# Sliding-window attention inside a decoder block: both key blocks of a query tile folded into one square per head

## The chip, the core and the metric

The kernel runs on one core of a Trainium2 chip. The metric is the device time of one launch in microseconds (us); the median of three runs of the kernel before is 1155.35 us (1154.95 to 1155.95). The core has five engines with a queue each, worked in order: PE (matrix products; PEld is its weight load), DVE (vector), ACT (scalar, activations), POOL (general vector work, SBUF only) and SP (issues DMAs). An instruction waits at the head of its queue until the semaphores that it names are reached, and everything behind it waits with it.

## What is computed

A decoder block on x of 1024 x 1024 in float32: RMSNorm, an input projection, a pooling mixer beside a sliding-window attention, gates, output projections and an MLP. The change lies in the attention alone:

```python
s = einsum('bnqhgd,bnkhd->bnhgqk', qb, kk) * scale      # kk: previous block and own block, 256 keys
rel = qi + BLOCK - kj                                   # BLOCK = WINDOW = 128
s = where((rel >= 0) & (rel < WINDOW) & has_prev, s, NEG_INF)
p = softmax(concatenate([s, sink], -1))[..., :-1]
o = einsum('bnhgqk,bnkhd->bnqhgd', p, vv)
```

There are 8 tiles of 128 queries, 8 query heads of width 64, and 2 key/value heads. A query in row q of its tile sees keys q+1 to 127 of the previous block and keys 0 to q of its own: 128 keys at most, and for every key column j exactly one of the two blocks is visible.

## The kernel before

Every float32 operand of a matrix product is split into a high and a low part (`split`, L99: ACT copies the high part at L100, DVE or POOL subtracts at L101), and a product is three passes of parts (`PASSES`). Engine order is not written out by hand: a scheduler places the instructions by priority and readiness, and the tiles of a pool (a tag with so many buffers) add the waits for reuse.

The attention stage runs from about 45 to 154 us of the span. The loop at L489 goes over the query tiles n = 0 to 7 and works on two groups g of four heads each. For each (n, g):

- `score` (L279): 12 matmuls at L296 put the scores of four heads, 256 keys wide, into the two banks of tag "sc", of which there is one buffer. Four fused DVE instructions (L303) add the mask, scale and negate, write SBUF, and give the row minimum.
- `attend` (L307): ACT makes four exponentials with row sums (L318), DVE adds the sink, inverts and normalises all 4 x 256 columns (L322). PE transposes each head in two halves (L328: 8 transposes for n > 0, 4 for n = 0). For each key/value head ACT and DVE split the transposed 128 x 512 into parts (`pt`, L330). Twelve matmuls (L335) form the output, and ACT copies it out (L338).

Around it stand: `qkv_tile` (L340), the projections of tile n + 4 for n < 4 (L172, L178); `pre_qkv` (L242), which moves that projection out of PSUM on DVE (L247, L248) and applies the rotation on POOL (L255 to L258, "the rotation" below); `post_qkv` (L260), five transposes (L265, L266) and the splits of queries, keys and values, the values' subtraction on POOL; `make_rb` (L352), eight small matmuls; and `pool_u` (L509), whose 128 x 512 matmuls at L517 depend on nothing in the attention and are what the scheduler puts between the attention's matmuls once the projections have run out ("fillers" below). A stage later, at L703, POOL adds two 128 x 512 tiles in SBUF.

Of the kernel before, what the change touches and what calls it, by code (L numbers as in the profile page):

```python
# [8 lines left out]
F32 = mybir.dt.float32  # L9
F32R = mybir.dt.float32r  # L10
AF = mybir.ActivationFunctionType
ALU = mybir.AluOpType
AX = mybir.AxisListType

P = 128
S = 1024
# [4 lines left out]
NEG = -1e30  # L21
WINDOWS = (2, 4, 8, 16)
NH = 8
HD = 64
# [2 lines left out]
F = 4096  # L27
NF = F // P
HEAD_ORDER = (0, 4, 1, 5, 2, 6, 3, 7)


PASSES = ((0, 0), (0, 1), (1, 0))
# [3 lines left out]
C_MASK = C_ID + P  # L36
# [14 lines left out]
def block_kernel(ctx: ExitStack, tc, xt, x, consts, vecs, sinks, b_qkv, g_post, g_mlp, g_mlp_post,  # L51
                 w_qkv, w_u, w_g, w_pool, w_bp, w_ba, w_o, w_up, w_dn, x1_dram, spill, f_dram, out):
    nc = tc.nc
    act, dve, pool, pe = nc.scalar, nc.vector, nc.gpsimd, nc.tensor

    cp = ctx.enter_context(tc.tile_pool(name="cp", bufs=1))
# [11 lines left out]
    def nm(s):  # L68
        cnt[0] += 1
        return f"{s}_{cnt[0]}"  # L70
# [13 lines left out]
    def at(tag, bufs, shape, dt=F32):  # L84
        return ap_.tile([P] + shape, dt, tag=tag, name=nm(tag), bufs=bufs)

    def bank(tag, shape=None):
        return psum["pool"].tile([P] + (shape or [512]), F32, tag=tag, name=nm(tag), bufs=psum["bufs"][tag])
# [7 lines left out]
    def f32(ap):  # L96
        return ap.bitcast(F32)

    def split(hi, lo, src, eng=dve):  # L99
        act.copy(hi, src)  # L100
        eng.tensor_tensor(lo, src, f32(hi), ALU.subtract)  # L101
# [42 lines left out]
    cst = cp.tile([P, C_N], F32, name="cst")  # L144
    vec = cp.tile([P, V_N], F32, name="vec")
    snk = cp.tile([P, NH], F32, name="snk")
    nsnk = cp.tile([P, NH], F32, name="nsnk")
# [5 lines left out]
    warm = small(1, "warm")  # L153
    act.activation(warm, eps, AF.Identity)
    ident = cst[:, C_ID:C_ID + P]
    mask = cst[:, C_MASK:C_MASK + 2 * P]

    def bcast(src, n):
        t = bcp.tile([P, 1024], F32, tag="bc", name=nm("bc"))
# [23 lines left out]
    bq = {0: bq01[:, 0, :], 1: bq01[:, 1, :], 2: bank("mm"), 3: bank("mm")}  # L183
    bkv = {0: bank("at", [2, 256]), 2: bank("at", [2, 256])}
    bss = bank("at", [NT])
    sq = at("qkv", 2, [S])
    ones = vec[:, V_ONE:V_ONE + 1]
    for k in range(NK):
        xs = at("s4", 4, [S])
# [10 lines left out]
        q = wslot([2, 512]) if k < 6 else ga_.tile([P, 2, 512], F32R, tag="ga", name=nm("wq"))  # L200
        if k % 2 == 0:
            wkv.append(ga_.tile([P, 2, 2, 256], F32R, tag="ga", name=nm("wkv")))
        kv = wkv[-1]
        for th, t in enumerate(halves_):
            c = slice(th * 512, (th + 1) * 512)
# [24 lines left out]

    khi = at("khi", 1, [S], F32R)
    klo = at("klo", 1, [S], F32R)
    vs = {}
    y = [[None, None], [None, None]]
    for th in range(2):
        for kh in range(2):
# [3 lines left out]
    tfs = {}  # L240

    def pre_qkv(n):  # L242
        tf = y[1][n - 2].rearrange("p a b -> p (a b)") if n in (2, 3) else at("qkv", 2, [1024])
        tfs[n] = tf
        t = tf[:, :768].rearrange("p (h d) -> p h d", d=HD)
        rn = r1[:, n:n + 1]
        dve.scalar_tensor_tensor(tf[:, :512], bq[n], rn, bq_b[:, :512], ALU.mult, ALU.add)  # L247
        dve.scalar_tensor_tensor(tf[:, 512:768], bkv[n // 2 * 2][:, n % 2, :], rn, bq_b[:, 512:768], ALU.mult, ALU.add)  # L248
        c = cst[:, C_COS + 8 * n:C_COS + 8 * n + 8].unsqueeze(1).unsqueeze(1).broadcast_to([P, 10, 2, 8])
        s = cst[:, C_SIN + 8 * n:C_SIN + 8 * n + 8].unsqueeze(1).unsqueeze(1).broadcast_to([P, 10, 2, 8])  # L250
        rot = t[:, :10, :ROT].rearrange("p h (a b) -> p h a b", a=2)
        a = tf[:, 768:928].rearrange("p (h a b) -> p h a b", a=2, b=8)
        b = sp.tile([P, 10, 2, 8], F32, tag="rb", name=nm("rb"), bufs=1)
        eng = pool if n else dve
        eng.tensor_tensor(a, rot, c, ALU.mult)  # L255
        eng.tensor_tensor(b, rot, s, ALU.mult)
        eng.tensor_tensor(rot[:, :, 0, :], a[:, :, 0, :], b[:, :, 1, :], ALU.subtract)
        eng.tensor_tensor(rot[:, :, 1, :], a[:, :, 1, :], b[:, :, 0, :], ALU.add)  # L258

    def post_qkv(n):  # L260
        tf = tfs.pop(n)
        t = tf[:, :768].rearrange("p (h d) -> p h d", d=HD)
        bt, bk = (bank("at" if n < 2 else "mm") for _ in range(2))
        for m in range(4):
            pe.transpose(bt[:, m * P:(m + 1) * P], tf[:, m * P:(m + 1) * P], ident)  # L265
        pe.transpose(bk[:, :P], tf[:, 512:640], ident)  # L266
        qt = at("qt", 2, [2, 512], F32R)
        split(qt[:, 0, :], qt[:, 1, :], bt)
        ks = slice(n * P, (n + 1) * P)
        split(khi[:, ks], klo[:, ks], bk[:, :P])  # L270
        vt = at("v", 4, [2, 3, HD], F32R)
        pool.memset(f32(vt[:, :, 1, :]), 0.0)
        split(vt[:, 0, ::2, :], vt[:, 1, ::2, :], t[:, 10:12, :], pool)
        vs[n] = vt.rearrange("p l a d -> p l (a d)")
        qts[n] = qt

    scores, soft = {}, {}

    def score(n, g):  # L279
        qt = qts[n]  # L280
        k0 = max(n - 1, 0) * P
        nk = 2 * P if n else P
        msk = mask[:, 2 * P - nk:]
        s4 = at("s4", 4, [4, 256])
        if g == 0:
            soft[n] = tuple(sp.tile([P, NH], F32, tag=t, name=nm(t)) for t in ("nmx", "es", "den"))
        nmx = soft[n][0]
        sb = bank("sc", [2, 2, 256])

        with tc.high_priority():  # L290
            for i in range(2):
                m = 2 * g + i
                for j, (qx, kx) in enumerate(((0, klo), (1, khi), (0, khi))):
                    for kv in range(2):
                        r = slice(kv * HD, (kv + 1) * HD)
                        pe.matmul(sb[:, kv, i, :nk], qt[r, qx, m * P:(m + 1) * P], kx[r, k0:k0 + nk],  # L296
                                  start=j == 0, stop=j == 2)

        for i in range(2):
            for kv in range(2):  # L300
                j = 2 * i + kv
                h = 4 * g + j
                dve.tensor_tensor_reduce(s4[:, j, :nk], sb[:, kv, i, :nk], msk, -HD ** -0.5, nsnk[:, h:h + 1],  # L303
                                         ALU.add, ALU.min, nmx[:, h:h + 1])
        scores[n, g] = s4

    def attend(n, g):  # L307
        k0 = max(n - 1, 0) * P
        nkb = 2 if n else 1
        nk = nkb * P  # L310
        s4 = scores.pop((n, g))
        nmx, es, den = soft[n]
        gs = slice(4 * g, 4 * g + 4)
        dve.tensor_tensor(es[:, gs], snk[:, gs], nmx[:, gs], ALU.add)
        act.activation(es[:, gs], es[:, gs], AF.Exp)
        for j in range(4):
            h = 4 * g + j
            act.activation(s4[:, j, :nk], s4[:, j, :nk], AF.Exp, scale=-1.0, bias=nmx[:, h:h + 1],  # L318
                           accum_out=den[:, h:h + 1])
        dve.tensor_tensor(den[:, gs], den[:, gs], es[:, gs], ALU.add)  # L320
        dve.reciprocal(den[:, gs], den[:, gs])
        dve.tensor_tensor(s4[:, :, :nk], s4[:, :, :nk], den[:, gs].unsqueeze(2).broadcast_to([P, 4, nk]), ALU.mult)  # L322
        pts = []
        for kv in range(2):
            b = bank("at", [2, 2 * P])
            for kb in range(nkb):
                for i in range(2):
                    pe.transpose(b[:, kb, i * P:(i + 1) * P], s4[:, 2 * i + kv, kb * P:(kb + 1) * P], ident)  # L328
            pt = at("pt", 2, [2, 2, 2 * P], F32R)
            split(pt[:, 0, :nkb], pt[:, 1, :nkb], b[:, :nkb])  # L330
            pts.append(pt)
        yb = bank("at", [2, P])
        mms = [(kv, kb, j) for kv in range(2) for kb in range(nkb) for j in PASSES]
        for j, (kv, kb, (vh, ph)) in enumerate(mms):
            pe.matmul(yb.rearrange("p m q -> p (m q)"), vs[k0 // P + kb][:, vh, kv * HD:kv * HD + P],  # L335
                      pts[kv][:, ph, kb, :], start=j == 0, stop=j == len(mms) - 1)
        c = (n % 4) * P
        act.copy(y[n // 4][g][:, :, c:c + P], yb)  # L338

    def qkv_tile(n):  # L340
        bq[n] = bank("mm")
# [189 lines left out]
    d = {}  # L531
# [464 lines left out]
    sq = sp.tile([P, 2, NT], F32, tag="fsq", name="fsq", bufs=1)  # L996
# [90 lines left out]
    u, v, c11, c12 = acc4("u"), acc4("v"), acc4("c11"), acc4("c12")  # L1087
# [5 lines left out]
    for j, (i, s_) in enumerate(steps):  # L1093
# [12 lines left out]
        for t in range(4):  # L1106
# [18 lines left out]
            else:  # L1125
                n = 4 + t
# [18 lines left out]
def _layout(inputs):  # L1145
    a = {k: np.asarray(v) for k, v in inputs.items()}
    f = np.float32
    c = np.ascontiguousarray
    w_in, b_in = a["w_in"][0], a["b_in"][0]
    q = w_in[:, 512:1024].reshape(D, NH, HD)[:, HEAD_ORDER, :].reshape(D, 512)  # L1150
    bq = b_in[512:1024].reshape(NH, HD)[list(HEAD_ORDER)].reshape(512)

# [4 lines left out]
    x = a["x"][0]  # L1157
    consts = np.zeros((P, C_N), f)
    consts[:, C_ID:C_ID + P] = np.eye(P, dtype=f)
    rel = np.arange(P)[:, None] + P - np.arange(2 * P)[None, :]  # L1160
    consts[:, C_MASK:C_MASK + 2 * P] = np.where((rel >= 0) & (rel < P), 0.0, NEG)
    inv = f(THETA) ** (-np.arange(0, ROT, 2, dtype=f) / f(ROT))
    ang = np.arange(S, dtype=f)[:, None] * inv[None, :].astype(f)
    for col, t in ((C_COS, np.cos(ang)), (C_SIN, np.sin(ang))):
# [11 lines left out]
        ("x", x.reshape(NT, P, D)),  # L1176
        ("consts", consts),
        ("vecs", c(vecs)),
        ("sinks", c(a["attn_sinks"][0][list(HEAD_ORDER)])),
        ("b_qkv", c(np.concatenate([bq, b_in[1024:1280]]))),  # L1180
        ("g_post", a["g_mix_post"][0]),
        ("g_mlp", a["g_mlp_pre"][0]),
# [30 lines left out]
```

## Time and profile before

| | |
|---|---|
| median of 3 runs | 1155.35 us |
| the profiled execution's own time | 1155.82 us |
| its span, first to last instruction | 1154.0 us |
| mean granted PE clock over the span | 0.996 |
| PE idle in 40 to 160 us, by windows of 20 us | 2.13, 0.22, 0.73, 0.88, 0.21, 0.05 us |
| POOL busy in 60 to 160 us | 9.1 us of 100 |

A row of the page's groups gives line, engine, operation, output<-input, shape and count, then the busy time, the mean of one in ns, and the idle time of the engine just before them with what ended it. A row of the windows gives the busy time of each engine in a stretch and the granted PE clock as a share of full speed. A matmul's record lasts until its result is out, so that records overlap; what one costs PE's queue is the spacing of starts, which the timeline shows.

### The profile page before, as it was taken

What the parts mean: (1) busy time and instruction counts of PE and PEld (TensorE: products, weight loads), DVE (VectorE), ACT (ScalarE), POOL (GpSimd) and SP (SyncE); (2) the same over time, 40 slices, a digit from 0 to 9 for tenths busy, and PEclk for the clock granted to TensorE, in tenths of its full rate; (3) what the DMA queues carried; (4) which work ended last, traced back from release to release, by engine and by line L of the source; (5) the groups of instructions that cost most, each with busy time, mean ns of one, the idle gap of its engine ahead of it and who ended that gap; (6) DMA issues with size and microseconds to landing.
All of it is one profiled execution on the core that took longest, in us unless ns stands there. A gap on an engine that the chain in (4) does not pass through costs nothing.

```text
span 1154.0 us, 14409 instructions
## 1 busy us (share of the span) xinstructions
PE 1131.8 (98%) x5356; PEld 937.4 (81%) x5356; DVE 826.6 (72%) x1339; ACT 535.0 (46%) x927; POOL 49.1 (4%) x66
## 2 busy tenths in 40 slices
PE   7999999999999999999999999999999999999997
PEld 6878888788888887888788888888888888888885
DVE  7787979888654584776997766666657945446887
ACT  7465845544332233464655444444444345344342
POOL 3410100000000150000000000000000000000000
PEclk9999999999999999999999999999999999999999
DMA  7101243544345453333255434343788665432652
GB/s 263 62 1 55 75 144 119 187 170 147 121 169 184 149 198 110 128 128 128 91 219 215 160 145 163 139 169 133 263 302 285 218 198 175 135 93 73 201 189 104
DMA packets 66167, 179.10 MB, mean 155 GB/s; under 512 B 6193, under 2 KB 6193, under 8 KB 66097
## 3 DMA queue, kind: packets, MB, share of 16 engines
q1 hardware_dynamic: 60336, 157.73, 40.3%
q10 hardware_dynamic: 5760, 20.45, 4.6%
q8 instruction: 42, 0.69, 0.2%
q14 instruction: 29, 0.23, 0.1%
HBM read 127.82 MB, written 50.33 MB: 154 GB/s over the span
## 4 chain that ended last, share of the span: by engine, by line
PE 88%; DVE 5%; ACT 4%; DMA 2%; issue 1%; SPq 0%; DVEq 0%; ACTq 0%
PE mm L436 20%; PE at L436 16%; PE at L1051 14%; PE mm L1051 11%; PE mm L768 5%; PE mm L373 5%; PE mm L517 4%; PE mm L172 3%; PE mm L375 2%; PE at L335 2%; PE sc L172 1%; PE at L178 1%; PE sc L296 1%; ACT s L318 1%; PE at L328 1%
## 5 line engine op out<-in xcount | busy, mean ns | idle before, releaser
L1051 PE MATMUL at<-ar,wh 128*128 128x512 f32 x744 | 169.6, 389 | 0.0
L1051 PEld LDWEIGHTS at<-ar,wh 128*128 128x128 f32 x744 | 139.6, 188 | 29.4 <-DVE ar L101 0.4
L1051 PE MATMUL mm<-ar,wh 128*128 128x512 f32 x576 | 131.0, 389 | 0.0
L100 ACT CAST wh<-st 128x512 fp32r<-128x512 f32 (+1 forms) x106 | 67.4, 643 | 128.9 <-PE mm L436 39.3
L1051 PEld LDWEIGHTS mm<-ar,wh 128*128 128x128 f32 x576 | 108.1, 188 | 22.5
L101 DVE TENSOR_TENSOR wh<-raw,wh 128x1024 fp32r<-128x1024 f32 x53 | 64.9, 1224 | 82.0 <-ACT wh L100 81.9
L100 ACT CAST wh<-raw 128x1024 fp32r<-128x1024 f32 x53 | 55.9, 1055 | 133.5 <-PE at L1051 61.8
L101 DVE TENSOR_TENSOR wh<-st,wh 128x512 fp32r<-128x512 f32 (+1 forms) x106 | 83.1, 789 | 19.8 <-ACT wh L100 17.4
L436 PE MATMUL mm<-gr,wh 128*128 128x512 f32 x300 | 72.4, 391 | 0.1
L436 PE MATMUL mm<-T,wx 128*128 128x512 f32 x288 | 67.5, 389 | 0.0
L436 PEld LDWEIGHTS mm<-gr,wh 128*128 128x128 f32 x300 | 56.0, 188 | 12.0 <-ACT g L833 0.5
L436 PEld LDWEIGHTS mm<-T,wx 128*128 128x128 f32 x288 | 54.1, 188 | 11.2
L436 PE MATMUL at<-T,wx 128*128 128x512 f32 x252 | 59.1, 389 | 0.0
L436 PEld LDWEIGHTS at<-T,wx 128*128 128x128 f32 x252 | 47.3, 188 | 9.8
L436 PE MATMUL mm<-x,wh 128*128 128x512 f32 x216 | 51.4, 391 | 0.5 <-ACT g L443 0.5
L101 DVE TENSOR_TENSOR ar<-B,ar 128x1024 fp32r<-128x1024 f32 x37 | 45.1, 1220 | 6.2 <-ACT ar L100 6.2
L436 PEld LDWEIGHTS mm<-x,wh 128*128 128x128 f32 x216 | 40.3, 188 | 9.7 <-ACT g L443 1.1
L517 PE MATMUL mm<-x,wh 128*128 128x512 f32 x192 | 47.7, 393 | 0.0
L436 PE MATMUL at<-gr,wh 128*128 128x512 f32 x183 | 44.4, 389 | 0.0
L100 ACT CAST ar<-B 128x1024 fp32r<-128x1024 f32 x37 | 38.8, 1050 | 7.9 <-DVE s L850 3.2
L685 DVE TENSOR_TENSOR g<-g,mm 128x512 f32<-128x512 f32 x32 | 20.5, 683 | 28.7 <-PE mm L375 28.6
L517 PEld LDWEIGHTS mm<-x,wh 128*128 128x128 f32 x192 | 35.4, 188 | 6.5
(345 smaller groups left out, 2243.2 us busy)
## 6 DMA issues: line engine op xcount, KB each, us to landing
raw<-f_dram SPq DMA_DIRECT2D x53, 512.0 KB, 3.7
f_dram<-g SPq DMA_DIRECT2D x30, 512.0 KB, 3.3
B<-in_w_dn_dram SPq DMA_DIRECT2D x24, 512.0 KB, 5.8
st<-in_w_up_dram SPq DMA_DIRECT2D x22, 512.0 KB, 3.8
f_dram<-g ACTq DMA_DIRECT2D x17, 512.0 KB, 2.6
st<-in_w_g_dram SPq DMA_DIRECT2D x16, 512.0 KB, 3.7
g<-spill_dram SPq DMA_DIRECT2D x16, 512.0 KB, 4.5
raw<-in_w_dn_dram SPq DMA_DIRECT2D x16, 512.0 KB, 4.6
```

Of the source, the lines that this page charges most:

```text
L100: act.copy(hi, src)
L101: eng.tensor_tensor(lo, src, f32(hi), ALU.subtract)
L172: pe.matmul(bq, xs_[k][n // 4][:, xh, n % 4 * P:(n % 4 + 1) * P], wq[k][:, h, :], start=k == 0 and j == 0, stop=k == NK - 1 and j == 2)
L178: pe.matmul(bkv[n // 2 * 2][:, n % 2, :], xs_[k][n // 4][:, xh, n % 4 * P:(n % 4 + 1) * P], wkv[k // 2][:, h, k % 2, :], start=k == 0 and ...
L335: pe.matmul(yb.rearrange("p m q -> p (m q)"), vs[k0 // P + kb][:, vh, kv * HD:kv * HD + P], pts[kv][:, ph, kb, :], start=j == 0, stop=j == ...
L373: pe.matmul(bs[th], whi[:, k, :], rhs(k, hl, th), start=k == 0 and hl == 0, stop=False)
L375: pe.matmul(bs[th], wlo[:, k, :], rhs(k, 0, th), start=False, stop=k == nk - 1)
L436: pe.matmul(b, w[:, wh, kt, :], xo[kt][:, xh, :], start=not after and kt == 0 and j == 0, stop=kt == 3 and j == 2, skip_group_check=after)
L517: pe.matmul(b, (whi, wlo)[h][:, k, :], xr(k, xh, th), start=k == 0 and j == 0, stop=k == NK - 1 and j == 2)
L685: dve.tensor_tensor(z[:, sl], z[:, sl], bs[th], ALU.mult)
L768: pe.matmul(obs[n][dj], l, wos[k][whl][:, dj * 512:(dj + 1) * 512], start=k == 0 and hl == 0 and whl == 0, stop=k == NK - 1 and hl == 1)
L1051: pe.matmul(bs[t], fo[fh][:, k2, t * P:(t + 1) * P], wo_[wh][:, k2, :], start=not after and s2 == 0 and k2 == 0 and j == 0, stop=s2 == NS ...
```

## The change

The scores of both blocks are still computed, 256 wide. Then ACT copies the own block's 4 x 128 columns out of PSUM, and one DVE instruction (`copy_predicated`) overwrites the columns above the diagonal with those of the previous block (for n = 0 with a constant). From there on each head has one square of 128 x 128: a row maximum and its scaling on DVE, the exponentials on 128 columns, one normalisation of 4 x 128 columns, four transposes and one split. The output is formed as p times the previous block's values, plus (p masked to the own block) times (own values minus previous values). The masked copies `pc` of both parts are made by two POOL multiplications of 128 x 512, and the difference `dvs` is made and split on POOL and ACT in `post_qkv`. The number of matmuls into the output stays 12 (6 for n = 0); they stand in the order p high, p low, pc high, pc low. The order of heads inside a group, the constants and some buffer counts follow suit.

```diff
-    mask = cst[:, C_MASK:C_MASK + 2 * P]
+    from_prev = cst[:, C_MASK:C_MASK + P].bitcast(mybir.dt.uint32)
+    own_t = cst[:, C_MASK + P:C_MASK + 2 * P]
+    neg = cp.tile([P, 1], F32, name="neg")
+    dve.memset(neg, NEG)
...
     def post_qkv(n):
...
+        if n:
+            dt_ = at("dv", 3, [2, 3, HD], F32R)
+            dv = tf[:, 768:896].rearrange("p (a d) -> p a d", d=HD)
+            pool.tensor_tensor(dv, t[:, 10:12, :], tfs.pop(n - 1)[:, 640:768].rearrange("p (a d) -> p a d", d=HD),
+                               ALU.subtract)
+            pool.memset(f32(dt_[:, :, 1, :]), 0.0)
+            split(dt_[:, 0, ::2, :], dt_[:, 1, ::2, :], dv, pool)
+            dvs[n] = dt_.rearrange("p l a d -> p l (a d)")
...
     def score(n, g):
...
-        s4 = at("s4", 4, [4, 256])
+        s4 = at("sc4", 4, [4, P])
...
-        for i in range(2):
-            for kv in range(2):
-                j = 2 * i + kv
-                h = 4 * g + j
-                dve.tensor_tensor_reduce(s4[:, j, :nk], sb[:, kv, i, :nk], msk, -HD ** -0.5, nsnk[:, h:h + 1],
-                                         ALU.add, ALU.min, nmx[:, h:h + 1])
+        heads = sb.rearrange("p a b k -> p (a b) k")
+        act.copy(s4, heads[:, :, nk - P:nk])
+        prev = heads[:, :, :P] if n else neg.unsqueeze(1).broadcast_to([P, 4, P])
+        dve.copy_predicated(s4, from_prev.unsqueeze(1).broadcast_to([P, 4, P]), prev)
+        gs = slice(4 * g, 4 * g + 4)
+        dve.tensor_reduce(nmx[:, gs], s4, AX.X, ALU.max)
+        dve.scalar_tensor_tensor(nmx[:, gs], nmx[:, gs], -SCALE, nsnk[:, gs], ALU.mult, ALU.min)
...
-            act.activation(s4[:, j, :nk], s4[:, j, :nk], AF.Exp, scale=-1.0, bias=nmx[:, h:h + 1],
-                           accum_out=den[:, h:h + 1])
+            act.activation(s4[:, j], s4[:, j], AF.Exp, scale=SCALE, bias=nmx[:, h:h + 1], accum_out=den[:, h:h + 1])
...
-        dve.tensor_tensor(s4[:, :, :nk], s4[:, :, :nk], den[:, gs].unsqueeze(2).broadcast_to([P, 4, nk]), ALU.mult)
-        pts = []
-        for kv in range(2):
-            b = bank("at", [2, 2 * P])
-            for kb in range(nkb):
-                for i in range(2):
-                    pe.transpose(b[:, kb, i * P:(i + 1) * P], s4[:, 2 * i + kv, kb * P:(kb + 1) * P], ident)
-            pt = at("pt", 2, [2, 2, 2 * P], F32R)
-            split(pt[:, 0, :nkb], pt[:, 1, :nkb], b[:, :nkb])
-            pts.append(pt)
+        dve.tensor_tensor(s4, s4, den[:, gs].unsqueeze(2).broadcast_to([P, 4, P]), ALU.mult)
+        b = bank("at", [4, P])
+        for j in range(4):
+            pe.transpose(b[:, j], s4[:, j], ident)
+        pt = at("s4", 4, [2, 4, P], F32R)
+        split(pt[:, 0], pt[:, 1], b)
+        pc = None
+        if n:
+            pc = at("s4", 4, [2, 4, P], F32R)
+            for h in range(2):
+                pool.tensor_tensor(pc[:, h], f32(pt[:, h]), own_t.unsqueeze(1).broadcast_to([P, 4, P]), ALU.mult)
+        probs[n, g] = pt, pc
+
+    def attend_v(n, g):
+        pt, pc = probs.pop((n, g))
         yb = bank("at", [2, P])
-        mms = [(kv, kb, j) for kv in range(2) for kb in range(nkb) for j in PASSES]
+        parts = ((vs[n - 1], pt), (dvs[n], pc)) if n else ((vs[0], pt),)
+        mms = [(v, p, kv, j) for v, p in parts for kv in range(2) for j in PASSES]
+        mms.sort(key=lambda e: (e[1] is pc, e[3][1]))
```

More of the change, by code (lines that the diff above doesn't have):

```diff
@@ L29 @@
 HEAD_ORDER = (0, 4, 1, 5, 2, 6, 3, 7)
+SOFT_ORDER = (0, 1, 4, 5, 2, 3, 6, 7)
 PASSES = ((0, 0), (0, 1), (1, 0))
@@ L185, in block_kernel @@
     bss = bank("at", [NT])
-    sq = at("qkv", 2, [S])
+    sq = at("qkv", 4, [S])
     ones = vec[:, V_ONE:V_ONE + 1]
@@ L232, in block_kernel @@
     klo = at("klo", 1, [S], F32R)
-    vs = {}
+    vs, dvs = {}, {}
     y = [[None, None], [None, None]]
@@ L242, in pre_qkv @@
     def pre_qkv(n):
-        tf = y[1][n - 2].rearrange("p a b -> p (a b)") if n in (2, 3) else at("qkv", 2, [1024])
+        tf = y[1][n - 2].rearrange("p a b -> p (a b)") if n in (2, 3) else at("qkv", 4, [1024])
         tfs[n] = tf
@@ L260, in post_qkv @@
     def post_qkv(n):
-        tf = tfs.pop(n)
+        tf = tfs[n]
         t = tf[:, :768].rearrange("p (h d) -> p h d", d=HD)
@@ L275, in post_qkv @@
         qts[n] = qt
+        if n:
[6 more added lines that the diff above has]
+            dvs[n] = dt_.rearrange("p l a d -> p l (a d)")
     scores, soft = {}, {}
+    SCALE = HD ** -0.5
     def score(n, g):
@@ L282, in score @@
         nk = 2 * P if n else P
-        msk = mask[:, 2 * P - nk:]
-        s4 = at("s4", 4, [4, 256])
+        s4 = at("sc4", 4, [4, P])
         if g == 0:
@@ L297, in score, with attend_t @@
                                   start=j == 0, stop=j == 2)
-        for i in range(2):
-            for kv in range(2):
-                j = 2 * i + kv
-                h = 4 * g + j
-                dve.tensor_tensor_reduce(s4[:, j, :nk], sb[:, kv, i, :nk], msk, -HD ** -0.5, nsnk[:, h:h + 1],
-                                         ALU.add, ALU.min, nmx[:, h:h + 1])
+        heads = sb.rearrange("p a b k -> p (a b) k")
[5 more added lines that the diff above has]
+        dve.scalar_tensor_tensor(nmx[:, gs], nmx[:, gs], -SCALE, nsnk[:, gs], ALU.mult, ALU.min)
         scores[n, g] = s4
[L307 to L310, printed above, removed]
+    probs = {}
+    def attend_t(n, g):
         s4 = scores.pop((n, g))
@@ L334, in attend @@
-        for j, (kv, kb, (vh, ph)) in enumerate(mms):
-            pe.matmul(yb.rearrange("p m q -> p (m q)"), vs[k0 // P + kb][:, vh, kv * HD:kv * HD + P],
-                      pts[kv][:, ph, kb, :], start=j == 0, stop=j == len(mms) - 1)
+        dve.tensor_tensor(s4, s4, den[:, gs].unsqueeze(2).broadcast_to([P, 4, P]), ALU.mult)
[4 more added lines that the diff above has]
+        split(pt[:, 0], pt[:, 1], b)
@@ new lines, in attend_t @@
+        pc = None
[6 more added lines that the diff above has]
+        pt, pc = probs.pop((n, g))
+        yb = bank("at", [2, P])
+        parts = ((vs[n - 1], pt), (dvs[n], pc)) if n else ((vs[0], pt),)
+        mms = [(v, p, kv, j) for v, p in parts for kv in range(2) for j in PASSES]
+        mms.sort(key=lambda e: (e[1] is pc, e[3][1]))
+        for j, (v, p, kv, (vh, ph)) in enumerate(mms):
+            pe.matmul(yb.rearrange("p m q -> p (m q)"), v[:, vh, kv * HD:kv * HD + P],
+                      p[:, ph, 2 * kv:2 * kv + 2].rearrange("p i q -> p (i q)"), start=j == 0, stop=j == len(mms) - 1)
@@ L337, in attend @@
         c = (n % 4) * P
         act.copy(y[n // 4][g][:, :, c:c + P], yb)
+    def attend(n, g):
+        attend_t(n, g)
+        attend_v(n, g)
     def qkv_tile(n):
@@ L1159, in _layout @@
     consts[:, C_ID:C_ID + P] = np.eye(P, dtype=f)
-    rel = np.arange(P)[:, None] + P - np.arange(2 * P)[None, :]
-    consts[:, C_MASK:C_MASK + 2 * P] = np.where((rel >= 0) & (rel < P), 0.0, NEG)
+    consts[:, C_MASK:C_MASK + P] = np.triu(np.ones((P, P), f), 1)
+    consts[:, C_MASK + P:C_MASK + 2 * P] = np.triu(np.ones((P, P), f))
     inv = f(THETA) ** (-np.arange(0, ROT, 2, dtype=f) / f(ROT))
@@ L1178, in _layout @@
         ("vecs", c(vecs)),
-        ("sinks", c(a["attn_sinks"][0][list(HEAD_ORDER)])),
+        ("sinks", c(a["attn_sinks"][0][list(SOFT_ORDER)])),
         ("b_qkv", c(np.concatenate([bq, b_in[1024:1280]]))),
```

## The prediction

> **What bounds the kernel now.** I read the page first, then the windows of the attention stage, its groups by form, PE's waits, and timelines.
>
> ```profile
> PE 1131.8 (98%) x5356; PEld 937.4 (81%) x5356; DVE 826.6 (72%) x1339; ACT 535.0 (46%) x927; POOL 49.1 (4%) x66
> ```
>
> PE is busy almost throughout, so time goes only with PE's work or PE's waits. The stage to be changed, in windows of 20 us (length, then PE, PEld, DVE, ACT, POOL busy, clock, DMA share, GB/s):
>
> ```profile
> 80.00:100.00 20.00, 19.27 (x142) 16.59 (x140) 13.14 (x39) 11.61 (x37) 0.67 (x2) 1.00 0.00 1
> 100.00:120.00 20.00, 19.12 (x142) 16.24 (x141) 17.08 (x43) 11.87 (x32) 3.55 (x10) 1.00 0.39 133
> 120.00:140.00 20.00, 19.79 (x164) 16.86 (x164) 19.39 (x67) 17.88 (x63) 1.81 (x5) 1.00 0.16 54
> 140.00:160.00 20.00, 19.95 (x129) 17.07 (x126) 13.10 (x28) 11.18 (x25) 0.00 (x0) 1.00 0.31 106
> ```
>
> PE is full even where DVE is nearly full (19.39 of 20), because the scheduler has put L517 fillers between the attention's matmuls. POOL does nearly nothing. PE's waits from 40 to 230 us, first lines (total, times, longest):
>
> ```profile
> PE sc L296 <- DVE nmx L303: 2.1, 1, 2.1
> PE at L556 <- DVE ar L101: 1.0, 1, 1.0
> PE at L335 <- DVE pt L101: 0.9, 3, 0.3
> ```
>
> DVE's relief is worth the 2.1 and little more. What can be won is PE work; what can be lost is new PE waiting.
>
> **What goes.** For n > 0 each group has four transposes instead of eight: 14 x 4 = 56 fewer. Eight of them take 0.87 us of PE's queue (starts 75.87 to 76.74 in the timeline), 0.109 each: **-6.1 us**, all on the path. The output's matmuls stay at 12 of 0.129 us (eleven from 78.22 to 79.64). The small waits of L335 and L328 (0.9 + 0.2 + 0.2) are replaced by what I lay out below: **-1.3**. The 2.1 us wait for the first scores: the single "sc" buffer was held by the masking at L303, which stood in DVE's queue behind a sum of exponentials. For n = 0 the new score copy on ACT frees it; laying the first instructions out by their row durations, the second scores are copied by about 56.8 us instead of 58.6, but later small waits (0.5 and 0.3 us, for normalisation and split) appear: **-1.3**.
>
> **What is added off the path.** DVE per group, spaced by starts: before 4 x 0.40 (L303), 1.14 (L322), 2 x 0.60 (splits) and three small ones, about 4.3; after, one normalisation and one split of 0.60, the predicated copy and the maximum. The last two the trace does not show: from below 0.60 each, what any 128 x 512 DVE row here takes, from above 1.22, the 128 x 1024 row; I take 0.60, since they touch 512 columns. So 2.8 us, or 4.0 at the upper end, in a period of over 4 us: hidden by the lead of the scores, which run two groups ahead. ACT per group: exponentials spaced 0.39 instead of 0.50, one copy more, one cast less: 2.9 us, hidden as well. If DVE's cover fails it is 14 x 0.3 us, in the range.
>
> **What is added on the path: POOL.** In the built kernel's order every group has two multiplications of 128 x 512 on POOL between the split and the last six of the output's 12 matmuls. The nearest rows of POOL:
>
> ```profile
> L703 POOL TENSOR_TENSOR g<-g,g 128x512 f32<-128x512 f32 x12 | 17.5, 1479 | 284.0 <-DVE g L685 284.0
> L215 POOL TENSOR_TENSOR qkv<-qkv,s 128x1024 f32<-128x1024 f32 x6 | 14.8, 2463 | 22.2 <-ACT s L214 22.1
> L255 POOL TENSOR_TENSOR qkv<-qkv,cst 128x160 f32<-128x160 f32 x5 | 2.7, 537 | 21.3 <-DVE qkv L248 20.3 <-issue 0.9
> ```
>
> L703 has the very shape; its minimum is 1285 ns, its median 1298, its maximum 1746. I take 1.27 for one behind another (the last pair, 2.54 us together).
>
> Let T be the moment when PE has issued a group's fourth transpose. ACT's cast starts at T+0.25 (transposes issued from 146.12, cast at 146.81) and lasts 0.59; the high matmuls can go at T+0.87, the low ones after DVE's 0.69 at T+1.6. POOL starts at about T+0.92, ends the high product at T+2.2 and the low at T+3.5; PE can use them at **T+2.25 and T+3.55**.
>
> The last four groups, (6,0) to (7,1): after T the order has four fillers (0.91 at 0.227, the spacing of L517), four high matmuls (0.52), a transpose of the next group (0.11), two low (0.26): T+1.85. Wait 0.4; four pc-high matmuls to 2.77; wait 0.78; two pc-low to 3.81; three transposes of the next group: 4.14. The period holds 2.9 us of PE work and **1.2 us of waiting**: 4.8 for four groups. The six groups (3,0) to (5,1) have scores (0.91) and one to five fillers instead; laid out likewise they wait 1.05, 0.35, 1.35, 1.15, 1.1 and 1.45 us: 6.4.
>
> For n = 1 and 2 POOL's queue holds something ahead of the first product, the rotation for tile n + 4:
>
> ```profile
> 77.22 0.53 POOL L255 TENSOR_TENSOR qkv<-qkv,cst 128x160 f32<-128x160 f32 x1 [15.79 <-DVE qkv L248]
> 77.71 0.53 POOL L256 TENSOR_TENSOR rb<-qkv,cst 128x160 f32<-128x160 f32 x1
> 78.32 0.36 POOL L257 TENSOR_TENSOR qkv<-qkv,rb 128x80 f32<-128x80 f32 x1
> 78.63 0.36 POOL L258 TENSOR_TENSOR qkv<-qkv,rb 128x80 f32<-128x80 f32 x1
> ```
>
> It waits for DVE to move a projection whose last matmul stands just ahead of the transposes (T-0.44, +0.25, +0.48 of L248), so it runs from T+0.3 to T+2.1; then the high product to 3.35, the new subtraction of values (0.46, as the values' row of 128 x 128), the low product to 5.1. PE reaches pc high at T+1.8 and waits 1.6, reaches pc low at 3.9 and waits 1.25; the scores of tile 3 or 4 queue behind it. Twice 2.85 = 5.7. Groups (1,1) and (2,1) have over a microsecond of fillers and scores in front and do not wait.
>
> Together 4.8 + 6.4 + 5.7 = 16.9 us. PE is a little slower than spacings alone give: from 76.74 to 112.49 us, spacings and waits come to 33.7 of 35.75. That brings PE later to its waits, about 0.15 us per group: 16.9 - 14 x 0.15 = **+14.8**.
>
> **Contention.** Where L703 runs, DVE's subtractions with both inputs in SBUF stretch from 0.69 us to 1.4 to 1.55, and one of each POOL pair to 1.75, while DVE's L685 with one input in PSUM keeps 0.64:
>
> ```profile
> 399.64 1.28 DVE L685 TENSOR_TENSOR g<-g,mm 128x512 f32<-128x512 f32 x2 [2.42 <-PE mm L375]
> 400.84 1.46 DVE L101 TENSOR_TENSOR wh<-st,wh 128x512 fp32r<-128x512 f32 x1
> ```
>
> In the attention only the normalisation has both wide inputs in SBUF, one per group; an L703-like hit costs 0.45 us of POOL and at most 14 x 0.45 = 6.3. It must fall just on a product that PE awaits: **+1.0**. [...]
>
> **The clock.** Windows of 2 us around the old wait:
>
> ```profile
> 56.00:58.00 2.00, 0.55 (x6) 0.31 (x3) 0.87 (x7) 1.25 (x7) 0.00 (x0) 1.00 0.00 0
> 58.00:60.00 2.00, 1.32 (x16) 1.22 (x17) 1.64 (x8) 2.00 (x11) 0.32 (x1) 0.99 0.00 0
> 60.00:62.00 2.00, 1.87 (x8) 1.38 (x6) 2.00 (x6) 1.38 (x6) 1.36 (x4) 0.50 0.00 0
> 62.00:64.00 2.00, 2.00 (x10) 1.82 (x9) 2.00 (x11) 0.38 (x2) 0.00 (x0) 0.65 0.00 0
> ```
>
> After a stretch with PE about half busy the clock falls to 0.50 for about 3.4 us, which costs 1.7. If the old wait shrinks this may vanish (-1.7); the two stretches at n = 1 and 2, some 2.85 us of waiting in 5, may each bring one (+1.7). I take 0 and keep -1.7 to +3.4.
>
> [...]
>
> **The sum** against the profiled execution's own 1155.8 (span 1154.0 and 1.8 around it): 14.8 + 1.0 - 6.1 - 1.3 - 1.3 = +7.1, so 1162.9. The median of the runs shown is 0.5 below that execution: **1162** us. What follows the attention (PE full from 154 to 200 us, DVE at 19.7 of 20) shifts as a whole: the fillers not used inside are done after it.
>
> **Rivals.**
>
> - Forecast, PE waits for POOL's products: 1158 to 1167. Chance 0.55.
> - Waits hidden, kernel faster: the sign turns if one product is ready early enough. Each 0.1 us off a product takes about 0.2 us off a group, 2.8 us in all; below about 1.0 us a product, or with PE 0.5 us later per group than laid out, the transposes' 6.1 us win. At 0.7 us a product, only about 3 us of waits at n = 1 and 2 remain: 6.1 + 1.3 + 1.3 + 1.7 (clock) less 3 gives 1148. Against it: no POOL row of 512 columns is under 1.28. Chance of under 1153: 0.15.
> - Waits as large as the savings, 1153 to 1157.6: half of them are covered, because PE's order has more slack than spacings tell. 14.8 halved is 7.4, less 8.7, plus 1: 1155. Chance 0.12.
> - Contention on nearly every pair and the clock falling at n = 1 and 2: 1162 + 5 + 3.4 = 1170. For it: every L703 pair shows a long product except the last. Chance 0.10.
> - No clock fall anywhere, waits as laid out: 1160, inside the forecast's range. Chance 0.08.
>
> Faster by over 0.2%, which is about what a measurement can tell from no change (below 1153.0): 0.15. Within: 0.12. Slower (above 1157.7): 0.73. The range 1153 to 1170 leaves out the fast rival and the tail of the contended one; the likeliest case's own is 1158 to 1167.
>
> **What would show it.** Right: PE waits on POOL at the output's line, about 15 us in all, longest at n = 1 and 2 behind the rotation; products of 1.25 to 1.75 us; 64 transposes; DVE well under 19 of 20 in 120 to 140 us. Wrong: waits on POOL under 7 us; or PE waits on DVE's predicated copy or ACT's exponentials at the scores or transposes, which would mean that the softmax chain and not POOL is late.

## The result and the profile after

The changed kernel takes **1180.68 us** (median of 4 runs, 1179.44 to 1181.71), the kernel before 1155.15 on the same chip: a ratio of 1.0221, 95% interval 1.0203 to 1.0238. It is slower by 25.5 us; the forecast was +7.

The profiled execution spans 1178.4 us. The page's first part after:

```profile
PE 1143.7 (97%) x5300; PEld 934.7 (79%) x5300; DVE 818.2 (69%) x1244; ACT 530.3 (45%) x934; POOL 92.1 (8%) x115
```

There are 56 fewer matrix instructions, as expected, and PE is nevertheless busy for 11.9 us more. Less work that takes longer means that some of it runs more slowly, so I looked for two things: new waits, and slower instructions. The windows of the attention (columns as before) show the waits:

```profile
80.00:100.00 20.00, 17.80 (x118) 15.01 (x117) 9.67 (x20) 8.19 (x30) 8.33 (x13) 0.91 0.00 1
100.00:120.00 20.00, 17.88 (x118) 15.18 (x117) 12.29 (x24) 10.82 (x32) 8.32 (x13) 0.91 0.09 29
120.00:140.00 20.00, 15.94 (x129) 12.79 (x128) 16.96 (x31) 12.18 (x43) 13.97 (x19) 1.00 0.46 157
140.00:160.00 20.00, 16.57 (x110) 12.64 (x109) 13.87 (x30) 11.15 (x43) 11.04 (x11) 1.00 0.00 1
```

PE, full before, now loses 2 to 4 us in each, and the granted clock falls to 0.91 in two windows that had 1.00. PE's waits from 40 to 180 us:

```profile
PE at L361 <- POOL s L351: 8.9, 14, 1.3
PE sc L315 <- ACT sc L318: 3.6, 1, 3.6
PE at L361 <- DVE s L103: 2.2, 2, 1.2
PE at L272 <- DVE qt L103: 1.3, 1, 1.3
```

The first line is the mechanism that I forecast. The second takes the place of the old wait of 2.1 and is longer, although the step that caused the old one is gone.

All this is at the attention. The last output matmul ends at 154.1 us before and at 168.1 after; of the 24.4 us between the spans, some ten come later, where no instruction of the diff runs, the clock reads 1.00 and PE does not wait more. There one must look at the length of one instruction. A group of the output projection, before and after (last columns: busy us, mean ns, idle before):

```profile
L373 PE MATMUL mm<-yahi,wh 128*128 128x512 f32 x64 | 24.9, 389 | 0.0
```

```profile
L403 PE MATMUL mm<-yahi,wh 128*128 128x512 f32 x64 | 25.3, 396 | 0.0
```

The same instruction on the same shapes takes 7 ns longer. Starts say it more sharply: back to back they stand 226.67 ns apart before (mean of 88 in 400 to 420 us) and 233.34 after (86 in the same stretch). From 870 us on, in the last stage, both kernels have 226.67. Added over all back-to-back 128x512 matmuls after 160 us, what exceeds 226.67 ("the excess" below) is 0.6 us before and **12.2 us after**.

### The profile page after: what moved, and what is told of

Same layout as the page of the kernel before. It is cut to its first block, busy times and chain, and to the rows that moved or that the text cites. A ratio compares the mean times of both kernels' runs of the same rounds, so it can differ in the third digit from the quotient of the medians.

```text
span 1178.4 us, 14222 instructions
## 1 busy us (share of the span) xinstructions
PE 1143.7 (97%) x5300; PEld 934.7 (79%) x5300; DVE 818.2 (69%) x1244; ACT 530.3 (45%) x934; POOL 92.1 (8%) x115
## 4 chain that ended last, share of the span: by engine, by line
PE 88%; DVE 6%; POOL 3%; ACT 2%; issue 1%; DMA 0%; SPq 0%; DVEq 0%; ACTq 0%
PE mm L466 21%; PE at L466 16%; PE at L1081 14%; PE mm L1081 11%; PE mm L798 7%; PE mm L403 5%; PE mm L547 3%; PE mm L179 3%; PE mm L405 3%; POOL s L351 2%; PE sc L179 1%; PE at L798 1%; PE at L185 1%; PE at L361 1%; PE sc L315 1%
## 5 line engine op out<-in xcount | busy, mean ns | idle before, releaser
L103 DVE TENSOR_TENSOR wh<-raw,wh 128x1024 fp32r<-128x1024 f32 x53 | 64.8, 1223 | 81.5 <-ACT wh L102 81.5
L103 DVE TENSOR_TENSOR wh<-st,wh 128x512 fp32r<-128x512 f32 (+1 forms) x106 | 83.5, 796 | 19.0 <-ACT wh L102 16.7
L466 PEld LDWEIGHTS mm<-gr,wh 128*128 128x128 f32 x300 | 56.0, 188 | 12.4 <-ACT g L863 0.5
L466 PEld LDWEIGHTS mm<-T,wx 128*128 128x128 f32 x288 | 54.1, 188 | 11.7
L103 DVE TENSOR_TENSOR ar<-B,ar 128x1024 fp32r<-128x1024 f32 x37 | 45.1, 1218 | 9.3 <-ACT ar L102 9.3
```

The costliest lines, as they stand in the source:

```text
L466: pe.matmul(b, w[:, wh, kt, :], xo[kt][:, xh, :], start=not after and kt == 0 and j == 0, stop=kt == 3 and j == 2, skip_group_check=after)
```

## The experiments

**Is it the attention's after-effect, or where the tiles lie?** The diff adds a constant of 128 x 1, `neg`, to the first pool of SBUF's left side. In the built kernel that pushes every left-side tile (weights `wh` among them) up by 32 bytes, while the right-side tiles (`x`, `yahi`, `wohi`) stay. The slow groups are those with one operand on each side; `at<-ar,wh` of the last stage has both on the left. Three kernels:

before_tile: the kernel before, with only this.

```diff
+    neg = cp.tile([P, 1], F32, name="neg")
+    dve.memset(neg, NEG)
```

> The kernel before with one thing of the change: a constant column of 128 x 1 at the end of the constants' pool, which nothing reads. It pushes every tile of the left side up by 32 bytes. Theory A (place in SBUF): in the changed kernel the 128x512 matmuls after 160 us start 226.67 ns apart where weights and moving operand lie on the same side, and 233.33 where they lie on different sides; the sum of the excess there is 12.2 us against 0.6 before, so this kernel takes 1155 + 11.6 = about 1167 us, with the attention as before. Theory B (the slower matmuls follow from the changed attention: its stalls and clock falls leave TensorE slower for some 700 us): 1155, spacing 226.67 throughout.

Measured: 1165.4 us, ratio 1.0082 (1.0067 to 1.0098). The excess after 160 us is 11.8, the attention is as before (its end at 153.4), and the group shows the changed kernel's length:

```profile
L375 PE MATMUL mm<-yahi,wh 128*128 128x512 f32 x64 | 25.3, 396 | 0.0
```

Theory A holds: a column that nothing reads costs 9.7 us. (The excess grew by 11.2, and the time by less, because PE's idle time after 170 us fell from 4.4 us before to 3.4 here.)

before_both: the same, and a column at the edge of the right side.

```diff
+    rpad = ctx.enter_context(tc.tile_pool(name="rpad", bufs=1, side="right"))
+    dve.memset(rpad.tile([P, 1], F32, name="rp0"), 0.0)
```

> The same with one more column on the right side, so that the right side's tiles move by 32 bytes too. If what counts is that the two operands of a matmul lie alike (modulo 64 bytes): 1155 us and 226.67 ns, as before. If each operand's own place counts (a multiple of 64 bytes is bad): slower than the kernel with the left side moved alone, 1167 or more, since then all four kinds of pairs are on the bad place. Theory B: 1155 as well; this run tells only the two forms of A apart.

Measured: 1165.8, ratio 1.0084 (1.0069 to 1.0099), excess 12.3, so the expectation of "1155 if they lie alike" fell. But left tiles go up and right tiles grow downwards: the two sides were now 64 bytes out of step and not alike, except modulo 64. Pairs with both operands on one side were still fast (the last stage: 389 ns), so the place of each alone does not count either.

after_even: the changed kernel with a second column behind `neg`, left side up by 64 bytes.

> The changed kernel with a second constant column behind the first, which nothing reads: the left side lies 64 bytes up from before, so alike modulo 64. Theory A: the spacing after 160 us returns to 226.67 and the time falls by 11.6, to about 1169; what is left over the kernel before, some 14 us, is the attention's. Theory B: 1180, unchanged.

Measured: 1181.5, ratio 1.0216 (1.0196 to 1.0236), excess 12.7. My step of 64 bytes was wrong. Before, all the left and right tiles agree modulo 512, so the next runs moved the left side by larger steps: 512 bytes with the edit below, 256 and 128 with 64 and 32 columns in place of its 128.

```diff
-    neg = cp.tile([P, 1], F32, name="neg")
+    neg = cp.tile([P, 128], F32, name="neg")
...
-        prev = heads[:, :, :P] if n else neg.unsqueeze(1).broadcast_to([P, 4, P])
+        prev = heads[:, :, :P] if n else neg[:, :1].unsqueeze(1).broadcast_to([P, 4, P])
```

> The changed kernel with its constant column made 128 columns wide, of which the first is read: the left side lies 512 bytes up from before instead of 32. In the kernel before, the left and the right side's tiles lie alike modulo 512; moving one against the other by 32 or 64 bytes made the slow 233.33 ns spacing in every kernel so far. Theory A2 (what counts is that a matmul's two operands lie alike modulo 512 bytes or a divisor of it above 64): spacing 226.67 after 160 us, time 1181 - 11.6 = about 1169. Rival (the place itself counts, or only the 32 bytes step of before is good): spacing 233.33, 1181.

> The same with 64 columns: the left side 256 bytes up. Spacing 226.67 and about 1169 if 256 bytes (or 128) is the step that counts, 233.33 and about 1181 if it is 512. One look, for the spacing.

> The changed kernel with a constant of 32 columns: the left side 128 bytes up from before. With 256 and 512 bytes the spacing after 160 us was 226.67, with 32 and 64 it was 233.33. Spacing 226.67 and about 1169 to 1172 if 128 bytes is the step, 233.33 and about 1181 if it is 256. One look, for the spacing.

Measured: 512 bytes 1169.2, ratio 1.0114 (1.0097 to 1.0131), excess 0.7; 256 bytes 1172.0 (one run), excess 0.7; 128 bytes 1180.0 (one run), excess 11.9. The group with 512 bytes, and with 128:

```profile
L403 PE MATMUL mm<-yahi,wh 128*128 128x512 f32 x64 | 24.9, 389 | 0.0
```

```profile
L403 PE MATMUL mm<-yahi,wh 128*128 128x512 f32 x64 | 25.1, 392 | 0.0
```

So of the moves tried 256 bytes is the smallest without the price: with the two operands moved against each other by 32, 64 or 128 the spacing was 6.7 ns longer; by 256 or 512, not. PE's order of instructions is the same in the changed kernel and in these versions of it. From 1.0221 to 1.0114 is 1.07%, **12.4 us of the 25.5**. The excess fell by 11.6 (12.23 to 0.66). The granted clock differs as well, 0.989 to 0.995 in the runs of the changed kernel against 0.993 to 0.995 with 512 bytes, on the mean up to 3 us of the time; so the price of the move is known to a few us only. What in the chip does it stays open.

**ACT's queue.** This is ACT in the changed kernel just before the long wait for the first scores (start, duration, instruction, idle before and releaser):

```profile
54.28 0.30 ACT L102 CAST dv<-y 128x128 fp32r<-128x128 f32 x1 [1.94 <-POOL y L287]
54.49 0.29 ACT L102 CAST v<-y 128x128 fp32r<-128x128 f32 x1
57.65 0.30 ACT L102 CAST dv<-y 128x128 fp32r<-128x128 f32 x1 [2.88 <-POOL y L287]
57.86 0.58 ACT L318 COPY sc<-sc 128x512 f32<-128x512 f32 x1
```

The copy of the scores (0,0), which frees the one "sc" buffer, stands in ACT's queue behind the casts of two values' differences, and these wait for POOL's subtraction (L287), which stands behind POOL's rotations of tiles 2 and 3. The scores have been ready since 54.1. even_cast takes ACT out of that chain:

```diff
-            split(dt_[:, 0, ::2, :], dt_[:, 1, ::2, :], dv, pool)
+            pool.tensor_copy(dt_[:, 0, ::2, :], dv)
+            pool.tensor_tensor(dt_[:, 1, ::2, :], dv, f32(dt_[:, 0, ::2, :]), ALU.subtract)
```

> The kernel with the second column, and the high half of the values' difference written by POOL instead of ACT. Theory C: the 3.58 us wait for the first scores' copy comes from ACT's queue, which stood 1.94 and 2.88 us at the two casts of the differences of tiles 2 and 3, behind POOL's rotations; with the cast on POOL the copy of the second scores runs about 3 us earlier, the wait falls under 1 us and the clock's first fall (two windows of 3.41 us at half speed, 3.4 us lost) goes: 5 to 7 us less than with the second column alone, about 1163. Rival: the wait comes from the exponential's table load and the single score buffer: no more than 1 us less.

Measured: 1173.7, ratio 1.0152 (1.0132 to 1.0172), 7.8 us less than after_even; the wait fell from 3.6 to 0.3. The fall of the clock behind it went too, but not all the others: the profile has 13.6 us at half speed from 40 to 170 us against 23.9 in after_even's, which accounts for 5.1 of the 7.8. Theory C holds on the wait; the gain is a little above the 5 to 7 expected because more falls went than the one behind the wait, which was partly chance (see the last section). The expected 1163 had counted on 1169 for after_even.

**POOL's products.** k512_dve is the 512-byte kernel with `pool.tensor_tensor(pc[:, h], ...)` of L351 on DVE:

```diff
-                pool.tensor_tensor(pc[:, h], f32(pt[:, h]), own_t.unsqueeze(1).broadcast_to([P, 4, P]), ALU.mult)
+                dve.tensor_tensor(pc[:, h], f32(pt[:, h]), own_t.unsqueeze(1).broadcast_to([P, 4, P]), ALU.mult)
```

> The 512-byte kernel with both own-block products of each group on VectorE instead of POOL. Theory D (the attention's loss is POOL's late products): PE's waits for POOL (9 us in the changed kernel, 14 times) go, the clock falls at 86 and 107 us go too (3.4 us), and DVE's small operations are no longer stretched by POOL: 10 to 13 us under the 512-byte kernel, so about 1157. Rival (the products are late wherever they run, or DVE has no room for 28 more of 0.6 to 0.7 us, 18 us in 100): waits on DVE at the output's line take their place and it gains under 4 us.

Measured: 1153.0, ratio 0.9976 (0.9964 to 0.9988): 16 us under the 512-byte kernel, more than expected, though the falls at 86 and 107 us that the expectation counted are not in the 512-byte kernel's profile. The products' line (min/median/max ns) in the changed kernel and here:

```profile
L351 POOL TENSOR_TENSOR s<-s,cst x28: 1255/1282/1298, 81.8 to 166.2; 128x512 fp32r<-128x512 f32 x28
```

```profile
L351 DVE TENSOR_TENSOR s<-s,cst x28: 675/682/1007, 81.2 to 152.0; 128x512 fp32r<-128x512 f32 x28
```

and its PE waits, which hold no product of L351 any more:

```profile
PE sc L315 <- ACT sc L318: 3.6, 1, 3.6
PE at L344 <- DVE sc L341: 0.8, 2, 0.5
PE at L361 <- ACT s L102: 0.5, 1, 0.5
PE sc L315 <- DVE den L340: 0.3, 1, 0.3
```

DVE has 28 products more to do, 19.2 us in all, and is busy for 19.2 of 20 us from 120 to 140, and still no wait of PE is put down to one of them (its weight loads wait 0.7 us for them in all). The rival falls. The edit changes one thing more: the scheduler lays out PE's queue otherwise from 84 us on, so that the 16 us are for the products' place and this order together.

k512_cast_defer keeps the products on POOL (cast on POOL, 512 bytes), and emits each group's output matmuls after the next group's transposes (the last group's, and the store of the first half of the attention's output, move behind accordingly):

```diff
     def attend(n, g):
         attend_t(n, g)
-        attend_v(n, g)
+        late.append((n, g))
+        if len(late) > 1:
+            attend_v(*late.pop(0))
...
```

> The 512-byte kernel with the values' difference cast on POOL (as tried already: 7.8 us less) and each group's output matmuls put behind the next group's transposes, so that the next scores, transposes and softmax stand between a product and its use. If POOL's products are late only because their use stands right behind them: the waits for POOL fall from 9 us to under 2, most clock falls go, and with the 6.1 us of transposes saved the kernel comes to 1148 to 1156. Rival (PE is short of other work in the attention anyway: the wait goes over to the scores or the transposes): 1158 to 1162, with waits on DVE and ACT in POOL's place.

Measured: 1167.2, ratio 1.0093 (1.0076 to 1.0109). Neither expectation met it: the waits for POOL did not shrink, and waits for DVE came on top.

```profile
PE at L362 <- POOL s L352: 10.1, 7, 2.2
PE at L345 <- DVE sc L342: 4.6, 5, 1.5
PE mm L273 <- DVE qt L103: 2.9, 1, 2.9
```

The scheduler now put the split of the next tile's values (v and dv) into POOL's queue between a group's two products, from 115.85 to 117.34 us:

```profile
114.65 1.26 POOL L352 TENSOR_TENSOR s<-s,cst 128x512 fp32r<-128x512 f32 x1
115.85 0.20 POOL L279 MEMSET v<- 128x128 f32 x1
116.02 0.46 POOL L103 TENSOR_TENSOR v<-qkv,v 128x128 fp32r<-128x128 f32 x1
...
117.34 3.72 POOL L352 TENSOR_TENSOR s<-s,cst 128x512 fp32r<-128x512 f32 x3
```

So a later place in the emitted order did not help; whether an order written out by hand would, was not tried.

**Both repairs.** k512_cast_dve has the 512 bytes, even_cast's edit and k512_dve's.

> The 512-byte kernel with both repairs: the own-block products on VectorE, and the high half of the values' difference cast on POOL. With the products on VectorE alone the time was 1153.0 (0.998 of before), and what stood out was the 3.6 us wait for the first scores' copy and a clock fall right behind it (1.7 us). If ACT's queue behind POOL is the cause of both: 1153.0 - 3.3 - 1.7 = about 1148, and faster than the kernel before by 0.7%. Rival (POOL, which then casts seven times more, brings the differences late to the groups of tile 1, or VectorE's queue is the limit there): 1152 or more.

Measured: **1147.3**, ratio 0.9923 (0.9909 to 0.9937), faster than both kernels. The page's line and ACT at the place shown above:

```profile
PE 1123.8 (98%) x5300; PEld 929.6 (81%) x5300; DVE 825.6 (72%) x1272; ACT 528.5 (46%) x927; POOL 62.7 (5%) x94
```

```profile
53.05 0.59 ACT L319 COPY sc<-sc 128x512 f32<-128x512 f32 x1 [0.62 <-PE sc L316]
...
56.41 0.56 ACT L319 COPY sc<-sc 128x512 f32<-128x512 f32 x1
```

The first copy runs as soon as PE is done, 4.8 us earlier than in the changed kernel (1.1 of them because the scores are ready earlier), and the clock never falls between 40 and 170 us.

## Why the prediction was right and wrong

Undone one after the other, the parts of the 25.5 us are (differences of ratios, times 1156):

| part | measured, us | forecast, us |
|---|---|---|
| operands out of step (after to after_512) | +12.4 ± 2.8 | 0 |
| products on POOL (after_512 to k512_dve) | +16.0 ± 2.4 | +15.8 |
| ACT's cast behind POOL (k512_dve to k512_cast_dve) | +6.1 ± 2.1 | 0 |
| the rest of the change (k512_cast_dve to before) | -8.9 ± 1.6 | -8.7 |

The ± adds the two ratios' half intervals in squares. No other order of undoing was tried, and the clock's falls are shared out among the parts.

- **Right as a sum: the savings** (-6.1, -1.3, -1.3). 64 transposes are left, and without the three side effects the change gains 8.9. That it comes so near to 8.7 is partly luck: before loses 1.7 us to the fall of the clock at 60 us and k512_cast_dve has no fall, which I had put at 0, while PE's idle time from 40 to 170 us falls from 4.2 us to 2.8 only, 1.4 for the two terms of 1.3. Even the time of the second scores' copy holds there: by 56.8 us forecast, 56.41 to 56.97 measured.
- **Right in sum, by luck: POOL** (14.8 + 1.0). The mechanism is the forecast one, but the terms inside were off and made up for each other. The waits on POOL are 8.9 us and not 14.8: 1.3 and 0.9 at n = 1 and 1.13 and 0.90 at n = 2, against 1.6 and 1.25 laid out. PE's idle time by the records is the larger account: from after_512 to k512_dve it falls from 14.5 to 1.9 us between 60 and 170 us (9.7 of it on POOL there, 2.2 on a split of DVE that POOL holds up). Between 40 and 60 us it falls by 1.4 as well, but that is not the products', the first of which runs at 81 us: in k512_dve's execution a half-speed window from 45.1 us stretched the matmuls ahead of a wait for DVE. So some 3 us of the 16.0 are in no wait. Each wait cuts a run of matmuls whose last record lasts 0.28 us where starts stand 0.129 apart, and a dozen waits and more went; that would account for it, but no run shows it.
- **Wrong in kind: the contention.** From L703's rows I read a stretch of both engines' operations, 0.45 us of POOL a hit. Here DVE's small operations show a block. DVE and POOL around 131 us in the changed kernel:

```profile
131.12 1.27 DVE L334 TENSOR_TENSOR es<-snk,nmx 128x4 f32<-128x4 f32 x1
132.31 0.68 DVE L103 TENSOR_TENSOR s<-at,s 128x512 fp32r<-128x512 f32 x1
...
133.30 1.59 DVE L341 TENSOR_TENSOR sc<-sc,den 128x512 f32<-128x512 f32 x1
```

```profile
131.09 1.28 POOL L351 TENSOR_TENSOR s<-s,cst 128x512 fp32r<-128x512 f32 x1
133.06 1.28 POOL L351 TENSOR_TENSOR s<-s,cst 128x512 fp32r<-128x512 f32 x1 [0.70 <-DVE den L339]
```

  A sum of 128x4, 0.16 us in the median, starts 0.03 behind a product and ends 0.02 behind it. L341 begins within the second product, which ends at 134.34, and ends 0.55 after that. The split behind L334 comes a microsecond late, and PE waits 1.24 us for it (and 0.96 at the next such place, where L324 takes 1.26 behind the product of 136.25): the 2.2 us of `at L361 <- DVE s L103`. I had asked only whether POOL is delayed, and counted only wide DVE operations; here POOL came first and a four-column operation held the queue. What in the chip holds it no row shows. My reading of L703 was wrong on its own rows:

```profile
400.46 2.99 POOL L703 TENSOR_TENSOR g<-g,g 128x512 f32<-128x512 f32 x2 [271.69 <-DVE g L685]
```

  The first of these two lasts 1.29 us, to 401.75. DVE's subtraction of 1.46 us, begun at 400.84, ends at 402.30, 0.55 later. POOL's second, begun at 401.70, ends at 403.45, 1.15 after that. Each ends nearly its own length (0.69 and 1.29) after the one before it, as it would had it waited for it; what looked like a stretch of both fits a wait of each for the other. With the products on DVE, the wait of 2.2 us is gone.
- **Failed: "the 2.1 us wait for the first scores ... -1.3".** I laid out ACT's queue without the casts of dv that the new split puts into it. A split writes its high half on ACT even when its low half is given to POOL; I had counted POOL's instructions of that step and not ACT's, which is the one that blocks. With them the wait became 3.6 us instead of shrinking, two windows at half speed followed, and the part costs 6.1 us.
- **Failed, and the largest: "What follows the attention ... shifts as a whole".** I took instructions that the diff does not touch to be as long as before. 12.4 us came from a constant of four bytes a partition, listed in the diff and left without a term. Nothing in the profile of before showed the price, since there all operands agree; but that the constant moves every later tile could have been read off the built kernel, and an unknown price should have widened the range. With the operands in step the kernel takes 1169.2, just inside the range of 1153 to 1170 and 7 us above the forecast, for the reason of the point before.
- **The clock at 0.** In the changed kernel's profiled execution it fell at 55.4 (two windows), 86.2 and 106.6 us, 13.6 us at half speed against 3.4 before: up to 5.1 us more, part of the rival that I gave 0.10. In after_512's execution, with the same waits, only the two windows at 57.0 fell.

## What to carry to other kernels

When an edit adds a tile, ask what it moves: compare a group that the edit does not touch, by the mean of one instruction, before explaining anything else. When a helper issues on several engines, put each of its instructions into its engine's queue and ask what stands behind the one that waits. An engine that looks free, like POOL here at 4%, can be dear twice: its operation of 128x512 (L351) takes 1.28 us where DVE's takes 0.68, and the operations of DVE with two SBUF inputs that began beside it, in the rows above, ended only behind it, the 0.16 us sum among them.

## What the runs showed of the hardware

**Operands out of step.** Where moving operand and weights of this kernel's 128x512 fp32 matmuls were moved against each other by 32, 64 or 128 bytes, the next matmul started 233.3 ns later, by 256 or 512 bytes 226.67 (128 and 256 bytes in one execution each): 3% of such a matmul, and about 1% of this kernel's time.

**The clock's falls went by windows, not by single waits.** In the changed kernel's profile the clock reads 0.50 from 55.45 to 62.28, from 86.17 to 89.58 and from 106.65 to 110.06 us; the falls begin 30.72 and 20.48 us apart, nine and six times 3.413. In every profile they begin a whole number of 3.413 us after each other, in a grid whose place differs from execution to execution (its first line behind 42 us is at 42.90 in the profile of before and at 45.21 in the changed kernel's). Laying that grid over the eleven profiles that have a fall (40 to 170 us, windows behind a full-speed one), by the share of the window ahead that PE's records fill:

| PE busy in the window ahead | windows | of these followed by half speed |
|---|---|---|
| under 0.46 | 11 | 11 |
| 0.46 to 0.56 | 7 | 4 |
| 0.56 to 0.64 | 21 | 7 |
| 0.64 to 0.80 | 20 | 0 |
| over 0.80 | 325 | 3 |

The three of the last row lie at 44 to 45 us, behind the sixteen 128x1 matmuls of L234, whose records fill 1.95 us in k512_dve. So several waits of about a microsecond brought a fall where they shared a window: in the changed kernel PE was busy for 2.13 of the 3.41 us up to 86.16 (0.63), and the clock fell there. In after_512, with nearly the same waits, PE was busy for 1.79 of the 4 us from 82 to 86, and the clock stayed at 1.00 to 88: there a line of the grid, counted from the fall at 57.0, lies at 84.3, between them. The two profiles have four half-speed windows and two. That the place of the grid decides is my reading; no run moved the grid alone.
